# An encoder layer on one core: one RG-LRU pair moved behind the last head group, the first residual's affine per column block, three shared PSUM banks for small products, small loads on GpSimd's queue

## The chip, the core and the metric

The kernel runs on one core of one Trainium2 chip. A core has TensorE (PE in the profile, its weight loads PEld), VectorE (DVE), ScalarE (ACT), GpSimd (POOL) and SyncE (SP). Each executes its own list of instructions in order; they wait for one another through semaphores. SP, ACT and POOL also issue DMAs. SBUF holds the working tiles; PSUM, eight banks, takes the matmuls' results. The metric is the device time of one execution in microseconds (us); lower is better.

## The reference

One post-norm layer for 256 positions of width 2048, in fp32:

```
h  = LN(x)
z  = h @ w_in                                # u, gate | r,k,v + three small | gA | gB
yA = gelu(gate) * RGLRU(conv(u))             # 16 heads of 128: a linear scan in time
yB = RWKV7(r, k, v, decay, a, g)             # 32 heads of 64: a delta-rule recurrence
h  = LN1(ALPHA*h + (sig(gA)*yA + sig(gB)*yB) @ w_out)
h  = LN2(ALPHA*h + CrossAttn(h, mem))        # 4 heads, 256 memory tokens
h  = LN3(ALPHA*h + (silu(h@wg) * (h@wu)) @ wd)
```

The change touches the mixer (the second to fifth line) and the start of the fifth.

## The kernel before

**Weight tiles.** Every large product reads its weights once, in pieces of 128 x 1024 fp32 (512 KB). `split_half` (L148) loads a piece into `raw` from SP's queue (L152), lets ScalarE round it to `wh` (L155) and VectorE form the rest `wl` (L157). PE multiplies both parts: `wstat` (L162) with eight matmuls of 512 columns (L168) and eight of 256 (L171) a piece; `xstat` (L189), where the activations are the stationary side, with twelve of 512 (L202, L203, L206). A piece is called a unit below. `wtile` (L178) makes one tile of 128 output columns from two units, and ScalarE and VectorE join its two halves from PSUM (L183, L186: `jl`, `js`). `raw` has four buffers, `wh` and `wl` three, the accumulators two.

**Order.** The program is written in one order, and a planner makes from it, before the run, each engine's fixed list: among the instructions that it takes to be ready, the one of lowest priority number goes first. `stream` gives the weight pieces and their evacuations numbers by unit, ahead of all other work; `ahead` gives some loads the first place. `defer(n, fn)` (L79) writes `fn` into the program only after n more units, so small products fall between weight tiles. A new tile in a buffer waits until everything that used the old one is done.

**The mixer's loop** (L758) runs over four groups of four tiles (eight heads) of RWKV7. Per group:
- `rwkv_group` (L407): twelve weight tiles (k, r, v for each of four tiles, 24 units). Their small work (`tile_stage`, L437) goes into `kkr`, `gt`, `bkt` and `sv`, which have one buffer each for all groups; `zk`, `zr`, `zv` have two. The norm of the keys is a product in a bank of the pool `mixps` (L447), as are the two products of L502 that L506 masks into `gt`.
- three units later `recurrence` (L522): a triangular solve on VectorE in 31 steps (L547, L550), then DMAs that put its result into `ymat`. `PACE[g]` units after that, `chunk_steps` (L562): `x1z` (L565), small products into the pool `recps` (L571 to L628), and at its end the normalisation (L635 to L646), transposes (L655) and gate products (L662) with the weights `lwg`.
- `gate_group` of the group before (L735): four weight tiles, 8 units, with `yar` loaded back from DRAM.
- two `lru_pair`s (L668): six weight tiles each, 12 units, for two heads of the RG-LRU. The recurrent gates (L671) are two products into `lrups` (L674), a pool of one bank, read by ScalarE (L676, L678) into `rr` and `ii`, two buffers each; the scans (L722) follow five units behind the pair.
- the decay rates of the next group (L382) after 7 and 10 units, and their exponentials at the end of the second pair (`late`).

So the order is rwkv 0, pairs 0 and 2, rwkv 1, gate 0, pairs 4 and 6, rwkv 2, gate 1, pairs 8 and 10, rwkv 3, gate 2, pairs 12 and 14, gate 3. PSUM: two banks `mixps`, three `recps`, two accumulators, one `lrups`.

**After the loop** the twelve finished tiles of y are loaded as `yr` (L779, POOL's queue), behind the last chunk steps, whose memory they take. The residual `hres` is loaded (L801, POOL), scaled and shifted by the first LayerNorm's rows in `affine_rows` (L266): eight blocks of 256 columns, two buffers of `gb`, sixteen loads of 128 KB from ACT's queue (L272), 32 operations on VectorE (L274, L275). W_out is four column blocks of eight units; after each, `residual` (L790) adds the product. `mraw` (L814) loads the memory tokens for the attention into the tags vh0 and vh1.

Of the kernel before, what the change touches and what calls it, by code (L numbers as in the profile page):

```python
# [18 lines left out]
P = 128  # L19
# [8 lines left out]
NT = 16  # L28
NG = 4
DR = (7, 10)  # L30
PACE = (20, 28, 28, 16)
NB0, NB1 = 3, 5
XP, CP = 4, 5
ALPHA = float(2.0 ** 0.25)
# [12 lines left out]
def trunk(ctx, tc, x, memT, vec, rows, consts, lruw, loraw, w_in, w_out, wq, wk, wv, wo, wgu, wd, out,  # L47
# [4 lines left out]
    def dump(name, t):  # L52
        if name in dbg:
            nc.gpsimd.dma_start(dbg[name], t)
# [188 lines left out]
    def layer_norm(pre, st, gname, bname, psum, xh, xl, small, tags):  # L243
        mom = [ln_rstd(small, st, tt) for tt in range(2)]
        for nb in range(4):
# [7 lines left out]
            for k in range(4 * nb, 4 * nb + 4):  # L253
# [9 lines left out]
                eng = nc.gpsimd if k % 4 == 3 else nc.vector  # L263
                eng.tensor_tensor(xl[k], full, xh[k].bitcast(F32), ALU.subtract)

    def affine_rows(pre, gi, name):  # L266
        with tc.tile_pool(name=name, bufs=2) as pool:
            for nb in range(8):
                s = slice(nb * 256, (nb + 1) * 256)
                gb = pool.tile([P, 2, 256], F32, name="gb")  # L270
                for n in range(2):
                    nc.scalar.dma_start(gb[:, n, :], rows[gi + n:gi + n + 1, s].broadcast_to([P, 256]))  # L272
                for tt in range(2):
                    nc.vector.tensor_tensor(pre[:, tt, s], pre[:, tt, s], gb[:, 0, :], ALU.mult)  # L274
                    nc.vector.tensor_tensor(pre[:, tt, s], pre[:, tt, s], gb[:, 1, :], ALU.add)  # L275
# [7 lines left out]
    y_d = [dram.tile([P, T], F32, name=f"y_d{k}") for k in range(NT)]  # L283
    at = ExitStack()
    with ExitStack() as mx:
        mp = mx.enter_context(tc.tile_pool(name="mixps", bufs=2, space=PSUM))
        rp = mx.enter_context(tc.tile_pool(name="recps", bufs=3, space=PSUM))
        accs[0] = mx.enter_context(tc.tile_pool(name="accs", bufs=2, space=PSUM))
        lp = mx.enter_context(tc.tile_pool(name="lrups", bufs=1, space=PSUM))
        wk1 = mx.enter_context(tc.tile_pool(name="wk1", bufs=1, side="right"))  # L290
        bx = ExitStack()
        boot = bx.enter_context(tc.tile_pool(name="boot", bufs=1))
# [89 lines left out]
        def decay_rates(g, jp, rates):  # L382

            if jp == 0:
                rates.append(grp.tile([P, 4, T], F32, name="avg"))
                rates.append(grp.tile([P, 4, T], F32, name="evg"))
            avg, evg = rates
            lw = wk1.tile([P, 2, 2, P], F32, name="lw")
            nc.sync.dma_start(lw, loraw[2 * g + jp, :, 0:2])
            for n, dst in ((0, evg), (1, avg)):  # L390
                ps = mps()
                for jj in range(2):
                    nc.tensor.matmul(ps[:, jj * T:(jj + 1) * T], lw[:, n, jj, :], lo[n], start=True, stop=True)
                nc.scalar.activation(dst[:, 2 * jp:2 * jp + 2], ps.rearrange("p (j t) -> p j t", j=2), AF.Sigmoid)
            for j in range(2 * jp, 2 * jp + 2):
                nc.vector.tensor_tensor_scan(evg[:, j], cmask, evg[:, j], 0.0, ALU.mult, ALU.add)

        def decay_exps(avg, evg):
            dm = grp.tile([P, 4, 4], F32, name="dm", bufs=2)
            ev4 = evg.rearrange("p j (c t) -> p j c t", c=4)  # L400
            for j in range(4):
                nc.scalar.activation(dtg[:, j, :, 1:65], ev4[:, j], AF.Exp, scale=-CDEC)
            nc.vector.tensor_copy(dm, dtg[:, :, :, 64])
            nc.scalar.activation(evg, evg, AF.Exp, scale=CDEC)
            return avg, evg, dm
# [156 lines left out]
        def chunk_steps(g, kkr, gt, bkt, sv, dm, yb, gi):  # L562
# [85 lines left out]
            for j in range(4):  # L648
                i = 4 * g + j
                fs = slice(j * P, (j + 1) * P)  # L650
                lw = wk1.tile([P, 2, P], F32, name="lwg", bufs=2)
                nc.sync.dma_start(lw, loraw[i // 2, :, 2:4, i % 2])
                ps = rps()
                for a in range(2):
                    last = nc.tensor.transpose(ps[:, a * P:(a + 1) * P], ot[a][:, fs], ident)  # L655
                on = wk1.tile([P, T], F32, name="on", tag="A")
                nc.scalar.activation(on, ps[:, 0:T], AF.Identity, scale=col("gn_g", i), bias=col("gn_b", i))
                nc.vector.tensor_tensor(on, on, yb[:, j, :], ALU.add)
                ps = rps()
                with tc.issue_after(last.ins):  # L660
                    for a in range(2):
                        nc.tensor.matmul(ps[:, 0:T], lw[:, a, :], lo[2 + a], start=(a == 0), stop=(a == 1))  # L662
                nc.vector.tensor_tensor(yb[:, j, :], on, ps[:, 0:T], ALU.mult)
# [4 lines left out]
        def lru_pair(i0, late=None):  # L668
            st = []

            def recurrent_gates(i, uc, lrw):  # L671
                ps = lp.tile([P, 512], F32, name="lrups")
                for n in range(2):
                    nc.tensor.matmul(ps[:, n * T:(n + 1) * T], lrw[:, n, :], uc, start=True, stop=True)  # L674
                rr = wk1.tile([P, T], F32, name="rr", bufs=2)
                nc.scalar.activation(rr, ps[:, 0:T], AF.Sigmoid, bias=col("ba", i))  # L676
                ii = wk1.tile([P, T], F32, name="ii", bufs=2)
                nc.scalar.activation(ii, ps[:, T:2 * T], AF.Sigmoid, bias=col("bx", i))  # L678
                nc.vector.tensor_tensor(ii, ii, uc, ALU.mult)
                th = wk1.tile([P, T], F32, name="th", bufs=2)  # L680
                nc.scalar.activation(th, rr, AF.Tanh, scale=sp8[:, i:i + 1])
                st.append((i, rr, ii, th))

            for i in (i0, i0 + 1):
                lrw = wk1.tile([P, 2, P], F32, name="lrw", bufs=2)
                nc.sync.dma_start(lrw, lruw[:, i])
                ua = wk1.tile([P, T], F32, name="ur", tag="ge", bufs=2)
                wtile(w_in[52 + 3 * i], xTh, xTl, out=ua)
                uc = wk1.tile([P, T], F32, name="uc", bufs=2)
                with stream(32):  # L690
                    evac[0] = nc.scalar.activation(uc, ua, AF.Identity, scale=col("conv3", i),
                                                   bias=col("conv_b", i))
                    for s in (1, 2, 3):
                        nc.vector.scalar_tensor_tensor(uc[:, s:T], ua[:, 0:T - s], col(f"conv{3 - s}", i),
                                                       uc[:, s:T], ALU.mult, ALU.add)
                defer(4, partial(recurrent_gates, i, uc, lrw))
# [38 lines left out]
        def gate_group(g, yb):  # L735
            for j in range(4):
                i = 4 * g + j
                gb = wtile(w_in[100 + i], xTh, xTl)
                sb = wk1.tile([P, T], F32, name="sb", bufs=2)
                with stream(32):  # L740
                    nc.scalar.activation(sb, gb, AF.Sigmoid)
                nc.vector.tensor_tensor(sb, sb, yb[:, j, :], ALU.mult)
                yr = wk1.tile([P, T], F32, name="yar", bufs=2)
                with ahead():
                    nc.sync.dma_start(yr, ya_d[i])
                nc.vector.tensor_tensor(yr, sb, yr, ALU.add)
                if g < NG - 1:
                    with ahead():
                        nc.sync.dma_start(y_d[i], yr)
                else:  # L750
                    split_to(yr, yh[i], yl[i])
                dump(f"y{i}", yr)
# [4 lines left out]
            decay_rates(0, jp, rates)  # L757
        for g in range(NG):  # L758
            yb = rwkv_group(g, PACE[g], *(rates if g else decay_exps(*rates)))
            if prev is not None:  # L760
                gate_group(g - 1, prev)
            if g < NG - 1:
                rates, full = [], []
                defer(DR[0], partial(decay_rates, g + 1, 0, rates))
                defer(DR[1], partial(decay_rates, g + 1, 1, rates))
                lru_pair(4 * g)
                lru_pair(4 * g + 2, late=lambda: full.append(decay_exps(*rates)))
                rates = full[0]
            prev = yb
        lru_pair(NT - 4)  # L770
# [19 lines left out]
    def residual(nb, pt, st):  # L790
        for tt in range(2):
            s = hres[:, tt, nb * 512:(nb + 1) * 512]
            nc.vector.scalar_tensor_tensor(s, s, ALPHA, pt[tt], ALU.mult, ALU.add)
            ln_stats(st, hres, tt, nb)

    with at:
        ap_ = at.enter_context(tc.tile_pool(name="attn", bufs=1, reuse_waits="tile"))
        sm_ = at.enter_context(tc.tile_pool(name="attns", bufs=1, reuse_waits="tile"))
        for nb in range(4):
            s = slice(nb * 512, (nb + 1) * 512)  # L800
            nc.gpsimd.dma_start(hres[:, :, s], h0_d[:, :, s])  # L801
        affine_rows(hres, 0, "gb0")
        dump("h0", hres)
        st = ap_.tile([P, 2, 4, 6], F32, name="st1")
        for nb in range(4):
            pt = xstat([w_out[nb, u] for u in range(4)], yh, yl)
            residual(nb, pt, st)
        dump("pre1", hres)
        layer_norm(hres, st, "g1", "b1", mp, xTh, xTl, sm_, ("f0", "f1", "f2"))
# [223 lines left out]
```

## Time and profile before

| | us |
|---|---|
| median of three runs | 2167.06 |
| lowest and highest | 2162.23, 2167.65 |
| the profiled execution, of which the profile is | 2165.43 |
| its span, first to last instruction | 2163.6 |

| engine | busy, us |
|---|---|
| PE | 2085.8 |
| PEld | 1789.3 |
| DVE | 1476.9 |
| ACT | 1092.3 |
| POOL | 80.6 |

The profile is of one execution, its times in us from the first instruction. In a list of waits the columns are total, count and longest. In a table by stretches, each engine's busy time is followed by its number of instructions; the last three columns are the granted TensorE clock (1.00 is full speed), the DMA engines' busy share and GB/s. In a timeline the columns are start, duration, engine, line and operation, and in brackets the idle time before it and what ended it. In a list of groups the numbers behind the bar are busy us, mean ns, idle us before. A list of DMA issues ends with KB and the median us to landing.

### The profile page before, as it was taken

Reading aid. Unit: us, or ns where it says so; the run is one execution under the profiler, and the core shown is the slowest. Engines: PE = TensorE matmul, PEld = TensorE weight load, DVE = VectorE, ACT = ScalarE, POOL = GpSimd, SP = SyncE. Lnnn points to the kernel's source line nnn. Section 1 sums busy time; section 2 is a strip of 40 time slices with the busy share of each in tenths; the row PEclk is TensorE's granted clock in tenths of the full one; section 3 lists DMA queues with packets and bytes.
Section 4 is the critical chain, followed back from the end, with each engine's and each line's share of the span. In section 5 each row is a group of like instructions: output and inputs, shape, how many; then the busy total and the mean of one; then the engine's idle time right before and its main releaser. Section 6 shows DMA issues by size and latency. Waiting matters only on the chain.

```text
span 2163.6 us, 31791 instructions
## 1 busy us (share of the span) xinstructions
PE 2085.8 (96%) x12176; PEld 1789.3 (83%) x12176; DVE 1476.9 (68%) x2357; ACT 1092.3 (50%) x1656; POOL 80.6 (4%) x104
## 2 busy tenths in 40 slices
PE   7999999999999999988999999999999999999996
PEld 6888888888888888867878888788888888888885
DVE  7788877978796879667765565585555555544445
ACT  6756645565556555644644444355444444443332
POOL 1100010010001000110000000000000000000001
PEclk9999999999999999999999999999999999999998
DMA  8645535544554455467565544566555555555553
GB/s 287 198 156 178 173 108 158 178 142 151 159 182 133 150 162 194 132 215 238 186 207 192 170 140 166 192 204 202 187 187 192 187 188 192 186 192 193 193 192 125
DMA packets 148376, 387.75 MB, mean 179 GB/s; under 512 B 38784, under 2 KB 58112, under 8 KB 147712
## 3 DMA queue, kind: packets, MB, share of 16 engines
q1 hardware_dynamic: 137776, 368.81, 51.5%
q10 hardware_dynamic: 9296, 13.24, 2.3%
q0 software_dynamic: 1152, 3.67, 0.5%
q8 instruction: 95, 1.56, 0.3%
q14 instruction: 57, 0.47, 0.1%
HBM read 375.05 MB, written 10.62 MB: 178 GB/s over the span
## 4 chain that ended last, share of the span: by engine, by line
PE 82%; DVE 10%; DMA 4%; ACT 3%; issue 2%; POOL 0%; SPq 0%; ACTq 0%; DVEq 0%; POOLq 0%
PE acc L168 34%; PE acc L171 17%; PE acc L206 7%; PE acc L202 7%; PE acc L203 7%; DVE wl L157 4%; DMA gb<-in_rows_dram 2%; ACT wh L155 1%; DVE pd L547 1%; DVE xi L550 1%; PE rec L603 1%; PE rec L610 1%; PE rec L628 1%; PE mix L502 1%; PE rec L662 1%
## 5 line engine op out<-in xcount | busy, mean ns | idle before, releaser
L157 DVE TENSOR_TENSOR wl<-raw,wh 128x1024 fp32r<-128x1024 f32 x656 | 801.7, 1223 | 524.1 <-ACT wh L155 496.2
L155 ACT CAST wh<-raw 128x1024 fp32r<-128x1024 f32 x656 | 685.8, 1047 | 666.3 <-PE acc L203 262.4
L168 PE MATMUL acc<-xT,wh 128*128 128x512 f32 x3520 | 917.1, 399 | 5.7 <-DVE js L186 4.0
L168 PEld LDWEIGHTS acc<-xT,wh 128*128 128x128 f32 x3520 | 636.2, 190 | 123.8 <-DVE js L186 4.7
L171 PEld LDWEIGHTS acc<-xT,wl 128*128 128x128 f32 x3520 | 484.0, 191 | 36.0
L171 PE MATMUL acc<-xT,wl 128*128 128x256 f32 x3520 | 503.0, 284 | 0.0
L203 PE MATMUL acc<-wh,f 128*128 128x512 f32 x352 | 136.9, 389 | 0.0
L202 PE MATMUL acc<-wh,f 128*128 128x512 f32 x352 | 136.9, 389 | 0.0
L206 PE MATMUL acc<-wl,f 128*128 128x512 f32 x352 | 108.4, 389 | 0.0
L183 ACT COPY jl<-acc 128x256 f32<-128x256 f32 x236 | 86.6, 367 | 22.0 <-PE acc L171 20.1
L186 DVE TENSOR_TENSOR js<-acc,jl 128x256 f32<-128x256 f32 x215 | 90.0, 419 | 3.4 <-ACT jl L183 3.1
L206 PEld LDWEIGHTS acc<-wl,f 128*128 128x128 f32 x352 | 66.1, 188 | 13.7
L202 PEld LDWEIGHTS acc<-wh,f 128*128 128x128 f32 x352 | 66.1, 188 | 13.7
L203 PEld LDWEIGHTS acc<-wh,f 128*128 128x128 f32 x352 | 66.0, 188 | 13.7
L616 POOL TENSOR_SCALAR dms<-ct,dm 128x128 f32<-128x128 f32 x48 | 36.4, 771 | 787.3 <-DVE smat L622 712.7
L547 DVE TENSOR_TENSOR pd<-xi,al 128x2 f32<-128x2 f32 (+30 forms) x124 | 63.2, 510 | 2.5
L203 PE MATMUL acc<-wh,A 128*128 128x512 f32 x128 | 50.5, 396 | 0.5 <-DVE A L212 0.5
L202 PE MATMUL acc<-wh,A 128*128 128x512 f32 x128 | 50.3, 394 | 0.3 <-ACT A L211 0.3
L202 PE MATMUL acc<-wh,oT 128*128 128x512 f32 x128 | 50.0, 391 | 0.0
L203 PE MATMUL acc<-wh,oT 128*128 128x512 f32 x128 | 49.8, 389 | 0.0
L203 PE MATMUL acc<-wh,B 128*128 128x512 f32 x128 | 49.8, 389 | 0.0
L202 PE MATMUL acc<-wh,B 128*128 128x512 f32 x128 | 49.8, 389 | 0.0
(260 smaller groups left out, 2095.7 us busy)
## 6 DMA issues: line engine op xcount, KB each, us to landing
raw<-in_w_in_dram SPq DMA_DIRECT2D x232, 512.0 KB, 3.5
raw<-in_wgu_dram SPq DMA_DIRECT2D x176, 512.0 KB, 3.4
raw<-in_wd_dram SPq DMA_DIRECT2D x88, 512.0 KB, 3.6
raw<-in_wk_dram SPq DMA_DIRECT2D x32, 512.0 KB, 4.3
raw<-in_w_out_dram SPq DMA_DIRECT2D x32, 512.0 KB, 4.6
raw<-in_wv_dram SPq DMA_DIRECT2D x32, 512.0 KB, 3.5
raw<-in_wq_dram SPq DMA_DIRECT2D x32, 512.0 KB, 3.4
raw<-in_wo_dram SPq DMA_DIRECT2D x32, 512.0 KB, 3.4
```

The costliest lines, as they stand in the source:

```text
L155: nc.scalar.copy(h, raw)
L157: nc.vector.tensor_tensor(l, raw, h.bitcast(F32), ALU.subtract)
L168: nc.tensor.matmul(acc, w, both[id(xh[k])], start=(k == 0), stop=False)
L171: mm = nc.tensor.matmul(acc[:, 0:T], l[:, kk * P:(kk + 1) * P], xh[k], start=False, stop=(k == 15))
L183: nc.scalar.copy(t, a[:, T:2 * T])
L186: nc.vector.tensor_tensor(out, a[:, 0:T], t, ALU.add)
L202: nc.tensor.matmul(pt[tt], xh[k][:, ts], w, start=(first and kk == 0), stop=False)
L203: nc.tensor.matmul(pt[tt], xl[k][:, ts], w, start=False, stop=False)
L206: nc.tensor.matmul(pt[tt], xh[k][:, ts], l[:, kk * 512:(kk + 1) * 512], start=False, stop=(last and kk == 1))
L502: nc.tensor.matmul(pt[hh][:, c * P:(c + 1) * P], q["bk"][rows, c, :], kr[rows, c, :], start=True, stop=True)
L547: nc.vector.tensor_tensor(pd[:, 0:nj, 0:t + 1], xi[:, 0:nj, 0:t + 1], al[:, 0:t + 1, t].rearrange("p (o s) -> p o s", o=1) .broadcast_to([ ...
L616: nc.gpsimd.tensor_scalar(dms[:, j * P:(j + 1) * P], smask, dm[:, j, c:c + 1], None, ALU.mult)
```

## The change

Four things:
1. Pair 10 (heads 10 and 11) is issued after the tiles of group 3 and ahead of gate 2, in place of the second pair after gate 1. The exponentials for group 3 then hang on pair 8. `PACE` of groups 2 and 3 becomes 20.
2. The recurrent gates' products use `mixps`, which gets three banks; `lrups` is gone. `recps` is opened first and so has the banks ahead of it.
3. The loads of `lw`, `lwg`, `lrw` and `yar` are issued by GpSimd, not SP.
4. `affine_rows` for the first residual is replaced by two loads of whole rows, 1 MB each, spread over the partitions, from GpSimd's queue into the tags vh0 and vh1, and by `affine_block`, four operations of 512 columns ahead of each block's residual.

```
-PACE = (20, 28, 28, 16)
+PACE = (20, 28, 20, 20)
...
+    def affine_block(pre, g, b, nb):
+        s = slice(nb * 512, (nb + 1) * 512)
+        for tt in range(2):
+            nc.vector.tensor_tensor(pre[:, tt, s], pre[:, tt, s], g[:, s], ALU.mult)
+            nc.vector.tensor_tensor(pre[:, tt, s], pre[:, tt, s], b[:, s], ALU.add)
...
-        mp = mx.enter_context(tc.tile_pool(name="mixps", bufs=2, space=PSUM))
         rp = mx.enter_context(tc.tile_pool(name="recps", bufs=3, space=PSUM))
+        mp = mx.enter_context(tc.tile_pool(name="mixps", bufs=3, space=PSUM))
         accs[0] = mx.enter_context(tc.tile_pool(name="accs", bufs=2, space=PSUM))
-        lp = mx.enter_context(tc.tile_pool(name="lrups", bufs=1, space=PSUM))
...
-            nc.sync.dma_start(lw, loraw[2 * g + jp, :, 0:2])
+            nc.gpsimd.dma_start(lw, loraw[2 * g + jp, :, 0:2])
...
-                nc.sync.dma_start(lw, loraw[i // 2, :, 2:4, i % 2])
+                nc.gpsimd.dma_start(lw, loraw[i // 2, :, 2:4, i % 2])
...
-                ps = lp.tile([P, 512], F32, name="lrups")
+                ps = mps()
...
-                nc.sync.dma_start(lrw, lruw[:, i])
+                nc.gpsimd.dma_start(lrw, lruw[:, i])
...
-                    nc.sync.dma_start(yr, ya_d[i])
+                    nc.gpsimd.dma_start(yr, ya_d[i])
...
             yb = rwkv_group(g, PACE[g], *(rates if g else decay_exps(*rates)))
+            if g == NG - 1:
+                lru_pair(NT - 6)
             if prev is not None:
                 gate_group(g - 1, prev)
...
-                lru_pair(4 * g)
-                lru_pair(4 * g + 2, late=lambda: full.append(decay_exps(*rates)))
+                exps = lambda: full.append(decay_exps(*rates))
+                if g < NG - 2:
+                    lru_pair(4 * g)
+                    lru_pair(4 * g + 2, late=exps)
+                else:
+                    lru_pair(4 * g, late=exps)
...
-        affine_rows(hres, 0, "gb0")
-        dump("h0", hres)
+        gb0 = []
+        for n in range(2):
+            b = ap_.tile([P, 2048], F32, name="gb0", tag=f"vh{n}")
+            nc.gpsimd.dma_start(b, rows[n:n + 1, :].broadcast_to([P, 2048]))
+            gb0.append(b)
         st = ap_.tile([P, 2, 4, 6], F32, name="st1")
         for nb in range(4):
             pt = xstat([w_out[nb, u] for u in range(4)], yh, yl)
+            affine_block(hres, gb0[0], gb0[1], nb)
             residual(nb, pt, st)
```

## The prediction

> **What bounds the kernel now.** I read the page first, then PE's waits, then its stalls in slices of 4 us, then the timeline around each.
>
> ```profile
> span 2163.6 us, 31791 instructions
> PE 2085.8 (96%) x12176; PEld 1789.3 (83%) x12176; DVE 1476.9 (68%) x2357; ACT 1092.3 (50%) x1656; POOL 80.6 (4%) x104
> ```
>
> TensorE (PE) is the bound, and no part of the change takes matmuls out. What can be won is PE's idle time, 77.8 us, and the half-clock time behind each idle stretch. PE's waits, with total, count and longest in us, name the idle time:
>
> ```profile
> PE lrups L674 <- ACT ii L678: 12.2, 4, 3.6
> PE rec L662 <- DMA lwg<-in_loraw_dram: 7.4, 3, 6.4
> PE acc L206 <- DVE wl L157: 6.1, 4, 3.9
> PE acc L168 <- DVE js L186: 4.0, 3, 1.9
> PE mix L447 <- DVE gt L506: 3.4, 7, 0.5
> PE rec L655 <- DVE ott L646: 2.7, 1, 2.7
> ```
>
> All six lie in the mixer or in the W_out product. The unit of the argument is half a weight tile, split, multiplied and counted once:
>
> ```profile
> 663.33 2.00 PE L168 MATMUL acc<-xT,wh 128*128 128x512 f32 x8
> 665.17 1.11 PE L171 MATMUL acc<-xT,wl 128*128 128x256 f32 x8
> 666.12 2.00 PE L168 MATMUL acc<-xT,wh 128*128 128x512 f32 x8
> ```
>
> A unit takes 666.12 - 663.33 = 2.79 us and holds eight L168 matmuls, so L168 counts divided by 8 count units. The moved pair is 6 tiles, 12 units, 33.5 us of PE; it is only put elsewhere.
>
> **Third bank for the small products.** The recurrent gates' second product waits until ScalarE has read the first from the only lrups bank, and ScalarE is late because rr, two deep, waits for the scans of the pair before. Slices (PE's busy time first, DVE's third, then PEclk):
>
> ```profile
> 224.00:228.00 4.00, 1.57 (x5) 1.30 (x5) 4.00 (x7) 2.87 (x7) 0.00 (x0) 0.69 0.43 143
> 228.00:232.00 4.00, 4.00 (x15) 3.52 (x14) 3.84 (x7) 2.20 (x4) 0.00 (x0) 0.50 0.65 217
> 660.00:664.00 4.00, 4.00 (x17) 3.32 (x17) 2.71 (x6) 1.74 (x3) 0.00 (x0) 0.70 0.88 237
> 872.00:876.00 4.00, 4.00 (x18) 3.44 (x18) 2.58 (x5) 2.30 (x4) 0.00 (x0) 0.75 0.94 223
> 600.00:660.00 60.00, 54.02 (x298) 46.97 (x297) 58.65 (x108) 36.37 (x62) 0.00 (x0) 0.99 0.56 171
> ```
>
> Stalls 12.2 us plus slow clock behind three of them, 4 x (0.50 + 0.30 + 0.25) = 4.2: at most 16.4 us. With three shared banks the second product no longer waits for the first one's reader. But VectorE (DVE) is full in these stretches (58.65 of 60), its order is fixed, and the next wl comes when it comes; and the chunk steps behind stand just in time:
>
> ```profile
> 879.12 0.70 DVE L565 STREAM_TRANSPOSE x1z<-ymat 32x512 f32<-32x512 f32 x1
> 879.88 1.20 PE L571 MATMUL rec<-x1z,gt 128*32 128x32 f32 x32
> ```
>
> x1z is ready at 879.82 and PE uses it at 879.88: a PE that comes earlier waits here. I take half, **-8** (0 to -16.4). The key norm's wait (L447 on gt) is one for a mix bank; a third bank removes it: **-3** (0 to -3.4). That a gate now holds a mix bank while it waits for rr costs nothing, as two others stay free and L447's stage uses two.
>
> **The pair moved behind the last head group.** What it is to cover is the end of the mixer, where the last chunk steps run almost alone:
>
> ```profile
> 880.00:932.00 52.00, 20.08 (x72) 12.51 (x72) 1.00 0.41 130
> 932.00:947.00 15.00, 0.00 (x0) 0.00 (x0) 0.77 0.75 263
> 934.72 1.46 SPq L652 DMA_DIRECT2D lwg<-in_loraw_dram  x2
> 936.00:940.00 4.00, 0.00 (x0) 0.00 (x0) 2.36 (x6) 2.63 (x5) 0.00 (x0) 0.86 1.03 395
> 940.00:944.00 4.00, 1.62 (x4) 1.38 (x5) 0.00 (x0) 0.00 (x0) 0.00 (x0) 0.50 0.57 197
> 944.00:948.00 4.00, 3.20 (x10) 1.99 (x10) 3.27 (x9) 2.39 (x7) 0.00 (x0) 0.79 0.34 94
> ```
>
> The first two rows hold L168 alone: 72/8 = 9 units are left when the chunk steps of group 3 begin at 880, and none from 932 on. Then PE waits 2.7 us for the norm (L655) and 6.4 us for the gate weights lwg (L662), and runs at half clock: 9.1 us of waits, and 1.62 x 0.50 + 3.20 x 0.21 = 1.5 of clock, 10.6 in all. After the change 12 + 8 + 12 + 12 + 8 = 52 units follow group 3's tiles instead of 40, and chunk steps that start at a like distance find about 20 units. What is late next is lwg again: it is issued from GpSimd (POOL) behind 12 yr and 4 hres loads, so a few us of its wait may stay. I take **-7.5** (0 to -10.6).
>
> The cost is at the other end. Group 2 loses 12 units of cover, so its chunk steps fall into group 3's tiles:
>
> ```profile
> 566.00:669.00 103.00, 64.09 (x243) 44.75 (x242) 0.98 0.60 180
> 661.00 1.44 DVE L565 STREAM_TRANSPOSE x1z<-ymat 32x512 f32<-32x512 f32 x2
> 669.00:708.00 39.00, 12.16 (x41) 6.99 (x42) 1.00 0.33 107
> 252.17 1.20 PE L571 MATMUL rec<-x1z,gt 128*32 128x32 f32 x32 [0.22 <-DVE x1z L565]
> 289.63 0.45 DVE L475 TENSOR_TENSOR kkr<-zr,dtg 128x128 f32<-128x128 f32 x1 [1.31 <-PE rec L598]
> 280.00:300.00 20.00, 20.00 (x166) 17.17 (x165) 13.74 (x25) 8.89 (x14) 4.92 (x8) 1.00 0.24 81
> 740.00:760.00 20.00, 19.49 (x121) 16.59 (x121) 16.97 (x31) 10.13 (x17) 0.00 (x0) 1.00 0.38 132
> L157 DVE TENSOR_TENSOR wl<-raw,wh 128x1024 fp32r<-128x1024 f32 x656 | 801.7, 1223 | 524.1 <-ACT wh L155 496.2 <-PE acc L171 17.2 <-ACT rhsz L606 3.0
> ```
>
> Between 566 and 669 PE did 243/8 = 30 units; group 2's chunk steps then begin, x1z ready since 662.4. Gate group 1 and one pair are 20 units, so now they begin 9 to 10 units into group 3 (the new pace of 3 + 20 is no later bound). Group 3 may not write kkr, gt, bkt and sv, single buffers, until they are read: in group 0 the first write to kkr stood behind L598, 289.63 - 252.17 = 37 us after the start. In such a stretch PE also does 41/8 = 5 units, so the release comes at unit 15. The k, r and v tiles are two deep: the third r is due at unit 16. It just fits. But DVE, 16.97 of 20 us busy in a tile's plain stretch, then has two tiles' held work to catch up (its splits, wl, are 1.22 us each), so I charge **+3** (0 to +25, below). On the other side, group 2's solve gets no second pair beside it, and so loses one of the four lrups stalls, counted above.
>
> SP loses the loads lw, lwg, lrw and yar, and POOL gets them. Of these only lwg stands among the waits above; the others are issued long ahead. POOL's queue is short:
>
> ```profile
> L779 POOL DMA_DIRECT2D yr<-y_d x12: 537/538/739, 924.4 to 930.4; - x12
> lwg<-in_loraw_dram SPq DMA_DIRECT2D x16, 128.0 KB, 2.7
> yr<-y_d POOLq DMA_DIRECT2D x12, 128.0 KB, 4.1
> hres<-h_d POOLq DMA_DIRECT2D x4, 512.0 KB, 8.0
> gb<-in_rows_dram ACTq DMA_DIRECT2D x2, 1024.0 KB, 6.8
> ```
>
> The landing is 4.1 us against 2.7 for 128 KB, 1.4 later, with units to cover it: 0 (-2 for a freer SP, to +4).
>
> **A rule against it.** The Trainium skill, "SBUF — State Buffer", section "Who interferes with whom", says that descriptors of a GpSimd-issued load are not written while VectorE runs in a two-port mode, and advises the SP or ACT queue; the section on the bandwidth pool has 0.62 us grow to 3.1. By the page, an estimate: eight pairs of lwg 2.5 us late each, 20 us, and the sum would be near zero. The twelve yr issues above, 537 to 739 ns beside a working VectorE, show at most 0.2 us of it, and the page itself excepts operations with two inputs, as wl is. The sum keeps 0; the rule stands beside the third rival.
>
> **Affine per column block.**
>
> ```profile
> L274 DVE TENSOR_TENSOR hres<-hres,gb 128x256 f32<-128x256 f32 x48 | 19.3, 433 | 15.5 <-DMA gb<-in_rows_dram 13.3 <-issue 2.2
> 984.00:988.00 4.00, 2.57 (x9) 2.06 (x10) 4.00 (x6) 1.35 (x3) 0.00 (x0) 0.83 0.95 266
> 988.00:992.00 4.00, 4.00 (x15) 3.18 (x14) 4.00 (x10) 2.48 (x7) 0.00 (x0) 0.74 0.96 342
> ```
>
> Before, VectorE's queue stops again and again for 128 KB gb pieces, wl stands behind, and L206 loses 6.1 us plus 2.57 x 0.17 + 4.00 x 0.26 = 1.5 of clock: 7.6. Now 32 operations of 256 columns become 16 of 512, and two loads of 1 MB are waited for at most once each. The end of the mixer holds their place (tags vh), so they land about 8 to 12 us into W_out, an estimate from 8.0 and 6.8; the first residual needs them after 8 units, 22 us. If VectorE's order asks earlier, wl waits, with two spare units (5.6 us) before PE does. I take **-5** (-7.6 to +6). mraw now waits for the last block; 32 units of W_out cover its load, and none is charged.
>
> **Sum.** -8 - 3 - 7.5 + 3 + 0 - 5 = -20.5 us. The profiled execution took 2165.43 (span 2163.6 and 1.8 around it); it lies 1.6 under the median of the three runs. So 2165.4 - 20.5 = **2145**.
>
> **Rivals.** (1) *VectorE keeps the rhythm.* In the full stretches a vanished lrups stall becomes a wait for wl, js or x1z, and half of L447's too: the -8 and 1.5 of the -3 are lost. For it: DVE 58.65 of 60. Against: after 660 DVE has room (2.71 of 4) and PE still ran slow. Time: 2145 + 8 + 1.5 = 2154.5.
>
> (2) *Slower: group 3 stands behind group 2's chunk steps.* If the tiles run dry at unit 12 rather than 16, PE does 2.5 units instead of 5 in the chunk stretch (7 us idle), then waits for two tiles' held work: a tile's 16.97 less six wl of 1.22 leaves 9.6, and the joins are not held, so about 7 a tile, an estimate, and 14 us for two; 2 us of half clock; and the third solve starts 23 us later, which brings back the mixer's bare end, 7.5. That is 30.5 for the 3 charged: 2145 + 27.5 = 2172. It decides at the point where kkr's release passes unit 16. Against it: group 0's steps reach into group 1's tiles too, and PE waited 0.22 us at their start and was busy 20.00 of 20 from 280 to 300.
>
> (3) *POOL's loads come late.* lwg then lands between yr's 1.4 and hres's 5.3 us after the old 2.7, say 3 us that PE waits in each of the first three groups, and behind yr and hres in the last, where half of the 7.5 is lost: 2145 + 9 + 4 = 2158. For it: POOL issues in order, behind its own work and waits. Against: its issues above are steady. The Trainium skill's "SBUF — State Buffer" would have it so.
>
> (4) *Everything is covered*: all of the stalls go, nothing new: 2165.4 - 16.4 - 3.4 - 10.6 - 7.6 = 2127.
>
> **How the numbers follow.** Forecast 0.58 (2135 to 2152), rival 1 0.15, rival 2 0.10, rival 3 0.07, rival 4 0.10. A change under 0.3% (6.5 us) is what a measurement here can't tell from none. Faster: 0.58 + 0.10, 0.12 of rival 1 and 0.03 of rival 3 = 0.83; same: 0.03 + 0.04 and 0.03 of rival 2 = 0.10; slower 0.07. Range 2130 to 2162: it leaves out rival 2 and the ends of 4 and 3.
>
> **What would show it.** Right: no wait at the gates' product over 1 us; L447 gone from PE's waits; main units (L168) running beside the last L662; one idle stretch at most on L274's successor. Wrong: PE idle inside group 3's first two tiles with the releaser L598 or L628, or DVE; L662 waiting over 4 us for lwg; L206 waiting for wl with VectorE stopped at gb0. The sum is wrong altogether if the compiled order of VectorE shifts the solve, whose end sets when the chunk steps start.

## The result and the profile after

The changed kernel takes 2144.44 us (median of 4 runs, 2141.4 to 2147.81), the kernel before 2166.11 beside it (4 runs, 2162.23 to 2167.65): a ratio of 0.990 [0.9887, 0.9913]. Forecast was 2145.0. The profiled execution took 2147.81 us. Below, a ratio is also given in us, as its distance from 1 times 2166.1: here -21.7 [-24.5, -18.8].

The page of the changed kernel, its head:

```profile
span 2146.0 us, 31754 instructions
PE 2078.3 (97%) x12176; PEld 1782.4 (83%) x12176; DVE 1472.4 (69%) x2341; ACT 1092.3 (51%) x1658; POOL 117.4 (5%) x162
```

PE's idle time, span less busy, went from 77.8 to 2146.0 - 2078.3 = 67.7 us, and its busy time fell by 7.5 with the same 12176 matmuls. Together these are the 17.6 us by which the span is shorter.

Most of the 7.5 us is not slow clock. The products that are masked into `gt` (L502, now L507; 16 a tile, 256 in all) took PE 23.84 us and now take 18.59, 5.3 less. Eight of the sixteen go into one bank of `mixps`, eight into another. Two rows of the kernel before and one of the changed kernel:

```profile
360.02 1.16 PE L502 MATMUL mix<-kkr,bk 64*128 64x128 f32 x8
362.45 1.16 PE L502 MATMUL mix<-kkr,bk 64*128 64x128 f32 x8
...
357.18 1.16 PE L507 MATMUL mix<-kkr,bk 64*128 64x128 f32 x16
```

Where the two halves alternate, all sixteen take 1.16 us, as long as eight of one half alone. With two banks PE's list puts one half behind the other in 6 of the 16 tiles; with three, in none. The rest is about what the clock gives, an estimate: PE's busy time times the missing share of the clock, added up over slices of 4 us, fell from 14.2 to 11.6 us.

PE's waits in the changed kernel (line numbers are 5 higher than before in the mixer, so L576 is the old L571 and L667 the old L662):

```profile
PE acc L168 <- DVE m L330: 11.0, 2, 7.0
PE rec L576 <- DVE x1z L570: 10.5, 3, 4.4
PE acc L168 <- DVE js L186: 7.7, 6, 2.4
...
PE acc L202 <- ACT wh L155: 2.9, 1, 2.9
PE rec L667 <- DMA lwg<-in_loraw_dram: 2.4, 4, 0.8
...
PE acc L206 <- DVE wl L157: 1.0, 1, 1.0
```

Everything the change aimed at is gone or small: lrups (12.2), the key norm's L447 (3.4) and L655 (2.7) are no longer listed, lwg fell from 7.4 to 2.4, L206 from 6.1 to 1.0. That is 12.2 + 3.4 + 2.7 + 5.0 + 5.1 = 28.4 us of waits. Against it stand x1z with 10.5, js with 3.7 more (7.7 from 4.0) and wh with 2.9. The new rows are the subject of the experiments. (The m row, 9.0 before, lies in the start-up, which the change does not touch.)

### The profile page after: what moved, and what is told of

Same layout as the page of the kernel before. It is cut to its first block, busy times and chain, and to the rows that moved or that the text cites. A ratio compares the mean times of both kernels' runs of the same rounds, so it can differ in the third digit from the quotient of the medians.

```text
span 2146.0 us, 31754 instructions
## 1 busy us (share of the span) xinstructions
PE 2078.3 (97%) x12176; PEld 1782.4 (83%) x12176; DVE 1472.4 (69%) x2341; ACT 1092.3 (51%) x1658; POOL 117.4 (5%) x162
## 4 chain that ended last, share of the span: by engine, by line
PE 81%; DVE 10%; DMA 4%; issue 2%; ACT 2%; SPq 0%; POOL 0%; ACTq 0%; DVEq 0%; POOLq 0%
PE acc L168 33%; PE acc L171 17%; PE acc L206 7%; PE acc L202 7%; PE acc L203 7%; DVE wl L157 3%; DVE pd L552 1%; DMA gb<-in_rows_dram 1%; ACT wh L155 1%; DVE xi L555 1%; PE rec L608 1%; PE rec L633 1%; PE rec L615 1%; DMA mraw<-in_memT_dram 1%; PE mix L507 1%
## 5 line engine op out<-in xcount | busy, mean ns | idle before, releaser
L168 PE MATMUL acc<-xT,wh 128*128 128x512 f32 x3520 | 914.3, 399 | 10.0 <-DVE js L186 7.7
L168 PEld LDWEIGHTS acc<-xT,wh 128*128 128x128 f32 x3520 | 636.6, 190 | 128.8 <-DVE js L186 9.4
L206 PE MATMUL acc<-wl,f 128*128 128x512 f32 x352 | 108.4, 389 | 0.0
L183 ACT COPY jl<-acc 128x256 f32<-128x256 f32 x236 | 86.5, 367 | 24.5 <-PE acc L171 23.8
L203 PEld LDWEIGHTS acc<-wh,f 128*128 128x128 f32 x352 | 66.1, 188 | 13.8
L206 PEld LDWEIGHTS acc<-wl,f 128*128 128x128 f32 x352 | 66.1, 188 | 13.7
L913 ACT ACTIVATE fsg<-js 128x256 f32<-128x256 f32 x44 | 18.4, 417 | 55.7 <-DVE js L186 55.5
```

The lines of the kernel that those rows point to most:

```text
L168: nc.tensor.matmul(acc, w, both[id(xh[k])], start=(k == 0), stop=False)
L183: nc.scalar.copy(t, a[:, T:2 * T])
L203: nc.tensor.matmul(pt[tt], xl[k][:, ts], w, start=False, stop=False)
L206: nc.tensor.matmul(pt[tt], xh[k][:, ts], l[:, kk * 512:(kk + 1) * 512], start=False, stop=(last and kk == 1))
```

## Where the new waits stand

x1z is the solve's result, written to DRAM, read back and transposed; the chunk steps (L576) begin with it. Rows of the changed kernel's timeline at group 2's chunk steps and, in the last two, at group 3's:

```profile
636.19 0.69 DVE L555 TENSOR_REDUCE xi<-pd 128x16 f32<-128x512 f32 x1
636.91 1.27 SPq L558 DMA_DIRECT2D scx<-xi  x2
641.80 1.99 SPq L563 DMA_DIRECT2D ymat<-scx  x4
647.41 0.70 DVE L570 STREAM_TRANSPOSE x1z<-ymat 32x512 f32<-32x512 f32 x1
648.17 1.72 PE L576 MATMUL rec<-x1z,gt 128*32 128x32 f32 x32 [3.97 <-DVE x1z L570]
...
847.75 0.70 DVE L570 STREAM_TRANSPOSE x1z<-ymat 32x512 f32<-32x512 f32 x1 [2.71 <-DMA ymat<-scx]
848.51 1.92 PE L576 MATMUL rec<-x1z,gt 128*32 128x32 f32 x32 [4.43 <-DVE x1z L570]
```

The solve's last reduction ends at 636.9; its result is in x1z at 648.1, 11 us later. The four loads of L563 are issued from 641.80 to 643.30 and land 2.4 to 2.7 us after that, so by 646.0; the transpose begins at 647.41, behind other work in VectorE's list. So some 9 of the 11 us are the way through DRAM. At group 3 VectorE itself stands idle for the loads, 2.71 us. PE's queue already has L576 next: the list was fixed before the run, as if x1z were there by now, and the main products behind L576 can't pass it. So PE waits 3.97 us here and 4.43 us at group 3's steps (last row). Slices of 4 us around both (columns as in the prediction):

```profile
644.00:648.00 4.00, 0.20 (x1) 0.00 (x0) 3.90 (x8) 1.44 (x2) 0.54 (x1) 1.00 0.89 178
648.00:652.00 4.00, 3.83 (x37) 3.37 (x38) 1.95 (x3) 0.00 (x0) 0.00 (x0) 0.57 0.89 342
844.00:848.00 4.00, 0.08 (x1) 0.00 (x0) 1.29 (x2) 3.82 (x7) 0.00 (x0) 0.81 0.91 192
848.00:852.00 4.00, 3.49 (x36) 3.13 (x37) 3.97 (x8) 0.60 (x1) 0.00 (x0) 0.50 0.94 369
585.00:648.00 63.00, 57.76 (x320) 49.51 (x319) 61.80 (x125) 37.99 (x63) 2.16 (x4) 1.00 0.57 177
```

Each wait drags a slice at about half clock behind it: 3.83 x 0.43 + 3.49 x 0.50 = 3.4 us. The two heads cost 8.4 + 3.4 = 11.8 us. The last row shows with what the solve shares VectorE (third busy time): in the 63 us ahead of the chunk steps it has 1.2 us free, with solve, splits and gates in one queue. Whether x1z is late or PE early is seen below, beside a kernel without the move (e8).

## The experiments

Two theories. **A:** the parts add up, each by the stall that it removes. **B:** two parts (the moved pair, GpSimd's loads) remove the same stall at the end of the mixer, and the move pays for it again where the chunk steps begin. First each part alone on the kernel before, all on one chip, where that took 2167.83 us.

**Banks alone** (e1_banks)

```diff
-        mp = mx.enter_context(tc.tile_pool(name="mixps", bufs=2, space=PSUM))
         rp = mx.enter_context(tc.tile_pool(name="recps", bufs=3, space=PSUM))
+        mp = mx.enter_context(tc.tile_pool(name="mixps", bufs=3, space=PSUM))
-        lp = mx.enter_context(tc.tile_pool(name="lrups", bufs=1, space=PSUM))
...
-                ps = lp.tile([P, 512], F32, name="lrups")
+                ps = mps()
```

> Only the PSUM part of the change, on the kernel before: gates' products in mixps, three banks, no lrups. My theory: the four waits of the gates' second product (12.2 us) and the key norm's wait on gt (3.4) go, but some of the 16.4 us that hung on them comes back as waits for x1z at the head of the chunk steps: 2165.4 - 8 - 3, that is about 2155 (2151 to 2160). Rival, VectorE keeps the rhythm: nearly all of it comes back as waits for x1z, js or wl; 2160 to 2166. Rival, everything is covered: 2147.

Measured: 2150.66 us, ratio 0.9928 [0.9914, 0.9942], -15.6 us [-18.6, -12.6]. Rows of its waits:

```profile
PE rec L661 <- DMA lwg<-in_loraw_dram: 6.8, 2, 6.4
PE rec L570 <- DVE x1z L564: 6.7, 2, 3.3
PE acc L168 <- DVE js L186: 6.6, 4, 2.2
PE acc L206 <- DVE wl L157: 4.9, 3, 2.6
```

lrups is gone, and x1z and js have taken part of its place, lwg and L206 stay. The products into gt take 18.59 us here as well (L501), against 23.84. Still this is the largest part of the gain, and more than the 11 us forecast.

**The moved pair alone, with its PACE** (e2_move)

```diff
-PACE = (20, 28, 28, 16)
+PACE = (20, 28, 20, 20)
...
+            if g == NG - 1:
+                lru_pair(NT - 6)
...
-                lru_pair(4 * g)
-                lru_pair(4 * g + 2, late=lambda: full.append(decay_exps(*rates)))
+                exps = lambda: full.append(decay_exps(*rates))
+                if g < NG - 2:
+                    lru_pair(4 * g)
+                    lru_pair(4 * g + 2, late=exps)
+                else:
+                    lru_pair(4 * g, late=exps)
```

> Only the moved pair and its PACE, on the kernel before, with lrups still one bank. My theory: the bare end of the mixer goes (10.6 us), one of the four lrups waits goes with the pair that no longer stands beside the second solve, and 3 to 8 us come back as waits around the second and third chunk steps: 2156 to 2161. Rival, the move needs the third bank: nothing won, 2163 to 2170. Rival, group 3 stands behind the second chunk steps: over 2170, with PE idle inside group 3's first two tiles.

Measured: 2167.59 us, ratio 1.0006 [0.9995, 1.0017]: nothing. Rows of its waits:

```profile
PE acc L168 <- DVE js L186: 8.4, 7, 1.8
PE rec L571 <- DVE x1z L565: 6.7, 3, 3.5
PE lrups L674 <- ACT ii L678: 6.5, 2, 3.3
PE acc L206 <- DVE wl L157: 6.1, 3, 2.3
PE rec L662 <- DMA lwg<-in_loraw_dram: 6.0, 2, 5.4
```

L655 is gone and lrups halved, 2.7 + 5.7 us, but x1z comes in with 6.7 and js with 4.4 more. And lwg keeps its long wait, 5.4 us, although main products now follow the chunk steps: cover for PE does not bring the weights any earlier. SP issues this lwg at 910.47, behind POOL's yr and hres loads (this kernel's timeline):

```profile
899.18 6.57 POOL L785 DMA_DIRECT2D yr<-y_d  x12 [14.11 <-PE rec L628]
907.27 2.84 POOL L807 DMA_DIRECT2D hres<-h_d  x4 [1.52 <-ACT wh L155]
910.47 0.38 SPq L652 DMA_DIRECT2D lwg<-in_loraw_dram  x1
918.96 2.05 PE L662 MATMUL rec<-lo,lwg 128*128 128x256 f32 x4 [5.36 <-DMA lwg<-in_loraw_dram]
```

**The affine alone** (e3_affine): the diff's `affine_block` and its two loads in place of `affine_rows(hres, 0, "gb0")`, on the kernel before.

> Only the affine per column block with its two 1 MB loads, on the kernel before. My theory: the waits of L206 for wl in W_out (6.1 us and 1.5 of slow clock) fall to one stop of about 3 us: 2159 to 2163. Rival, the loads come late behind the bare end of the mixer, since they wait for the same memory: the stop is longer, 2164 to 2170.

Measured: 2157.23 us, ratio 0.9955 [0.9941, 0.9968], -9.7 us [-12.8, -6.9]. L206 stands no longer among the waits; those of the mixer stay, and grow a little in this profile (lrups 13.7, lwg 8.8, x1z 2.5).

**GpSimd's loads alone** (e4_pool)

```diff
-            nc.sync.dma_start(lw, loraw[2 * g + jp, :, 0:2])
+            nc.gpsimd.dma_start(lw, loraw[2 * g + jp, :, 0:2])
...
-                    nc.sync.dma_start(yr, ya_d[i])
+                    nc.gpsimd.dma_start(yr, ya_d[i])
```

(and likewise lwg and lrw)

> Only the small loads lw, lwg, lrw, yar on GpSimd's queue instead of SP's, on the kernel before. My theory: nothing on the path, within 3 us of the kernel before, 2163 to 2168; L662's wait for lwg at the end stays, 6 to 9 us. Rival, POOL's loads come late: 2171 to 2180, with L662 waiting for lwg over 2 us in every group. Rival, a freer SP feeds raw earlier: 2160 or less.

Measured: 2159.57 us, ratio 0.9966 [0.9953, 0.9978], -7.4 us [-10.2, -4.8]. Rows of its waits:

```profile
PE acc L206 <- DVE wl L157: 9.3, 2, 6.4
PE rec L662 <- DMA lwg<-in_loraw_dram: 3.3, 4, 1.3
```

The part that was forecast at nothing wins what the move was forecast to win: the list has lwg at 3.3 for 7.4, its longest wait 1.3 for 6.4, and L655 gone (L206 is up by 3.2 in this profile). In the changed kernel POOL issues as follows (start, duration):

```profile
904.14 0.76 POOL L657 DMA_DIRECT2D lwg<-in_loraw_dram  x1 [25.65 <-PE rec L660]
905.23 0.73 POOL L657 DMA_DIRECT2D lwg<-in_loraw_dram  x1 [0.33 <-PE rec L667]
905.96 6.41 POOL L790 DMA_DIRECT2D yr<-y_d  x12
912.36 2.88 POOL L812 DMA_DIRECT2D hres<-h_d  x4
```

In one queue lwg goes ahead of yr and hres, because it comes first in the program (in e4 too: 929.95 and 931.04, yr from 931.76); from two queues it came behind them. The rival of a freer SP, 2160 or less, fits the time as well: the raw loads of w_in land no sooner (3.6 us in the median, 3.5 before), but how the 7.4 us divide between the two causes is not shown.

**The changed kernel without the move** (e8_nomove; f2_nomove is the same kernel again, on the chip of f1_after, the changed kernel again)

```diff
-PACE = (20, 28, 20, 20)
+PACE = (20, 28, 28, 16)
...
-            if g == NG - 1:
-                lru_pair(NT - 6)
...
+                lru_pair(4 * g)
+                lru_pair(4 * g + 2, late=lambda: full.append(decay_exps(*rates)))
```

> The changed kernel without the moved pair: old order, old PACE, but three mix banks, affine per block and GpSimd's small loads. New theory N: the move is a loss here; it gives its price back at the bare end only, and that end is already mended by lwg on GpSimd's queue. The parts alone gave 17, 11 and 8 us; with 2 to 6 us that more than one of them claims, 2134 to 2140, below the changed kernel. My prediction's terms: the move is worth 4.5 us, so without it 2147 to 2151.

> The changed kernel itself, to stand on one chip beside the next three: 2141 to 2147.

> The changed kernel without the moved pair and with the old PACE once more, on the chip of the changed kernel. Theory N: the move costs 3 to 8 us, so this is that much below the changed kernel. Rival, the difference seen was between chips: within 2 us of it. The prediction's term: 4.5 us above it.

Measured: e8, which has the old PACE too, 2140.22 us (2138.3 to 2142.09), ratio 0.9883 [0.9865, 0.9900]. On the other chip f1, with the move, 2147.44 (2142.6 to 2152.42), 0.9916 [0.9898, 0.9935], and f2, without it, 2140.46 (2137.95 to 2144.75), 0.9885 [0.9864, 0.9906]. Twice the kernel without the move is ahead, by 0.0017 (3.7 us, the first pair of ratios, on two chips) and 0.0031 (6.7 us, on one chip). The intervals overlap, so the size is loose; that the move wins 4.5 us in place is out. So is e2's rival, that the move would win if it had the third bank. Rows of e8's waits, and of its timeline at group 2's chunk steps:

```profile
PE rec L576 <- DVE x1z L570: 5.9, 2, 3.3
PE acc L168 <- DVE js L186: 4.4, 3, 2.1
...
PE rec L667 <- DMA lwg<-in_loraw_dram: 2.6, 4, 1.2
...
656.25 1.92 PE L576 MATMUL rec<-x1z,gt 128*32 128x32 f32 x58
```

The end of the mixer is mended without a pair behind it: lwg 2.6, longest 1.2, L655 not listed. x1z and js cost 10.3 here and 18.2 with the move. That is theory B.

At group 2 the solve is no later with the move: its last reduction ends at 636.9 us in the changed kernel and at 636.7 in e8. But e8, like the kernel before, begins the chunk steps after 1416 matmuls of L168 (177.0 units), without a wait; the changed kernel after 1386 (173.2 units). PE comes 3.8 units earlier there. The place follows PACE: 1400 with 26 for group 2 (e5 below), 1448 with 32 (e6).

**The small loads back on SP** (e9_nopool): the inverse of e4's diff, on the changed kernel.

> The changed kernel with the small loads on SP's queue again. Theory: lwg is late again behind raw and the residual's loads, one wait of L662 of about 5 us with slow clock behind it although pair 14 and gate 3 could cover it: 2147 to 2153. Rival, the prediction's term of nothing: 2142 to 2146.

Measured: 2148.34 us, ratio 0.992 [0.9902, 0.9939], beside f1's 0.9916 on the same chip: no difference. Yet in its trace the wait is back:

```profile
PE rec L667 <- DMA lwg<-in_loraw_dram: 5.3, 2, 4.7
```

A wait of 4.7 us lies about at the edge of what these intervals (4 us each way) can tell; the trace settles who makes lwg late, the times do not settle what it is worth beside the move.

**Group 2's chunk steps later** (e6_late): rival 2 of the prediction, sought by force.

```diff
-PACE = (20, 28, 20, 20)
+PACE = (20, 28, 32, 20)
```

> The changed kernel with PACE of group 2 at 32: its chunk steps begin 15 units into group 3, and kkr comes free near unit 20, past the point (unit 16) from which my second rival decides. Rival 2 then holds: PE idle in group 3's second or third tile behind L598's and L628's successors or VectorE, 2152 to 2170. Against it, the planner fills PE with pair 10's units: no such idle time, 2139 to 2147.

Measured: 2144.16 us, ratio 0.9898 [0.9878, 0.9918], the same as the changed kernel's 0.990. The chunk steps begin at 671.2 in place of 648.2, and group 3's first write to kkr moves from 685.8 to 704.0. A join of group 3 does wait for it (ScalarE's row), but PE has other work throughout (the stretch of the chunk steps; from 640 to 780 its longest stop is 2.03 us, for lwg):

```profile
671.00:711.00 40.00, 40.00 (x466) 34.93 (x465) 21.14 (x38) 14.53 (x23) 8.65 (x13) 1.00 0.23 79
705.02 0.51 ACT L371 ACTIVATE zr<-js,omu 128x256 f32<-128x256 f32 x1 [2.32 <-DVE kkr L481]
```

So group 3 behind kkr's release has some 18 us to spare beyond what the change uses. The x1z wait of this head is gone too, but the time is not lower: x1z keeps 4.8 us at the other heads, and the key norm's product (L452) waits 3.7 us for ScalarE in group 3's first tile, at 637.3, which it did not before.

**The chunk steps of groups 0, 2 and 3 later** (e5_pace), and, to separate it from the move, the same without the move (f3_nomove_pace: e8's diff with PACE (26, 28, 28, 26) and the same two lines).

```diff
-PACE = (20, 28, 20, 20)
+PACE = (26, 28, 26, 33)
...
         lru_pair(NT - 4)
+        lru_pair(NT - 2)
         gx.close()
...
-        lru_pair(NT - 2)
         flush()
```

> The changed kernel with PACE (26, 28, 26, 33) and, so that the last chunk steps can be that late, pair 14 issued ahead of the residual's allocation. Theory: the chunk steps are planned 2 to 4 us before VectorE has the solve ready; two units later the three waits for x1z (10.5 us and some 3 of slow clock) go: 2131 to 2138. Rival, VectorE keeps the rhythm: the time comes back as waits for js and wl: 2141 to 2148.

> The changed kernel without the moved pair, with PACE (26, 28, 28, 26) and pair 14 issued ahead of the residual's allocation, so that the chunk steps of groups 0 and 3 are planned some 2 units later. Theory: the two x1z waits (5.9 us, 1 to 2 of slow clock) go, and no others come: 2131 to 2136, the best of all. Rival: with no pair behind group 3 the later chunk steps lengthen the bare end by as much as they save: 2138 to 2143.

Measured: e5 2136.85 us (2131.32 to 2137.56), ratio 0.9864 [0.9844, 0.9884], -29.5 us: the fastest with the whole solve. On the same chip it is 3.4 us below e8, and their runs do not overlap (e8 from 2138.3). f3 2141.82, 0.9893 [0.987, 0.9915], no better than f2 beside it (2140.46). Three places in the timeline of e5:

```profile
636.49 0.70 PE L452 MATMUL mix<-sq,ct 128*128 128x256 f32 x2 [3.73 <-ACT sq L450]
652.39 1.43 DVE L570 STREAM_TRANSPOSE x1z<-ymat 32x512 f32<-32x512 f32 x2
653.75 2.11 PE L576 MATMUL rec<-x1z,gt 128*32 128x32 f32 x64
827.01 0.70 DVE L570 STREAM_TRANSPOSE x1z<-ymat 32x512 f32<-32x512 f32 x1 [1.20 <-DMA ymat<-scx]
841.39 1.79 PE L576 MATMUL rec<-x1z,gt 128*32 128x32 f32 x54
```

Group 2's x1z arrives just as PE comes to it, at 653.8; group 3's is there at 827.7 and PE takes it at 841.4, with main products between; no x1z wait is left in this kernel's list, and js is down to 3.9. But the key norm's product now waits for ScalarE, 5.5 us in two stops: the first row stands 17 us ahead of group 2's chunk steps, in place of the 3.97 us there. And at group 3 it is the solve that is earlier: it begins at 761.9 us, after 1591 matmuls of L168, in the changed kernel at 776.8, after 1619. The chunk steps are put back by less, from 1793 to 1808. What holds group 3's solve in the changed kernel is not shown.

So among these kernels the moved pair wins only together with these edits, and later paces win nothing without the pair: in f3, too, a stop for ScalarE (2.9 us) stands where group 0's x1z wait was, and group 3's chunk steps stay where e8 has them, 232.0 units in, with 2.6 us of wait.

**Half of the solve** (e7_solve). The kernel leaves out every second step of the solve, so its results are not the layer's; it shows what the solve's length and its load on VectorE cost together.

```diff
-            for t in range(1, 32):
+            for t in range(1, 32, 2):
```

> The changed kernel with every second step of the triangular solve left out (16 of 31, half of VectorE's work on it). Theory: VectorE's load beside the solve makes the waits for x1z (10.5 us) and js (7.7), so both go nearly whole, with their slow clock: 2122 to 2130. Rival, the way of the solve's result through DRAM is what is late: the x1z waits stay, 2136 to 2144.

Measured: 2116.24 us, ratio 0.9781 [0.9754, 0.9807], -47.4 us, by the ratios 26 below the changed kernel. x1z and js are no longer listed, and a stretch ahead of the chunk steps reads

```profile
573.00:618.00 45.00, 45.00 (x255) 39.62 (x254) 39.40 (x76) 24.71 (x41) 1.61 (x3) 1.00 0.65 200
```

PE 45.00 of 45.00, VectorE 39.40 of 45 where it was 61.80 of 63. The way through DRAM is unchanged in this kernel, 11.2 us at group 2 (602.1 to 613.3), and does no harm, since the solve is done sooner: it takes 28.7 us in place of 51.9. Whether the whole solve on an emptier VectorE would do as well is not shown. In the profiled executions, 32.5 us apart, PE's idle time falls by 18.7 us, about x1z's 10.5 and js's 7.7 together, and its busy time by 13.8; 9.1 of that is slow clock (added up as above, from 11.6 to 2.5 us).

## Why the prediction was right, and where it was not

The time and its sign were right, the sum in its parts was not: alone, three parts won more than their terms, and the fourth, the move, won nothing alone and cost time in place. That these errors cancelled to about 1 us is luck.

| term | forecast, us | part alone, us | in place |
|---|---|---|---|
| third bank (-8 and -3) | -11 | -15.6 [-18.6, -12.6] | not run |
| moved pair (-7.5 and +3) | -4.5 | +1.3 [-1.1, +3.7] | +3.7 and +6.7 (after over e8, f1 over f2) |
| GpSimd's loads | 0 | -7.4 [-10.2, -4.8] | -0.9 (f1 over e9), within the interval |
| affine | -5 | -9.7 [-12.8, -6.9] | not run |
| sum | -20.5 | -31.4 | -21.7 measured |

- **Third bank.** Right: the gates' product waits nowhere, L447 on gt is gone, and part of the gain came back as waits for x1z and js, as "a PE that comes earlier waits here" said. Mis-sized: 11 was taken and 15.6 measured. The prediction held that idle time and half-clock time are what can be won; 5.3 us of the part lie in busy time that it put at nothing, the products into gt, which a third bank lets alternate.
- **"What is late next is lwg again: it is issued from GpSimd (POOL) behind 12 yr and 4 hres loads."** Wrong, and the root of two wrong terms. lwg goes ahead of both. So the loads, charged at 0, mend the end of the mixer by themselves (lwg and L655 fall by 6.8 us in e4's list, though L206 grows by 3.2), and the -7.5 was a stall that another part of the same diff had already removed. The move alone couldn't have won it either: with cover, lwg still waited 5.4 us (e2).
- **"+3" for VectorE's catch-up.** Not where it was put: PE did not stand idle behind kkr's release, not even when that came 18 us later (e6). By the lists of waits the price of the move lies at the hand-over from solve to chunk steps: x1z and js, 18.2 us with the move and 10.3 without. The step that failed is "now they begin 9 to 10 units into group 3 (the new pace of 3 + 20 is no later bound)": it took the start from where x1z had been ready, but the list follows PACE, and PE came 3.8 units sooner and waited. So one sign of being wrong did come: PE idle in group 3's first two tiles behind DVE, 3.97 us for x1z. The price is not shown wait by wait: e6, without this wait, is no faster. And since group 3's solve begins 28 matmuls of L168 later than in e5, some catch-up of VectorE may stand behind the 4.43 us at group 3; no run separates this. The prediction had quoted the very rows (x1z at 879.82, PE at 879.88), and drew from them a limit to the banks' gain only, not a price of the move.
- **Affine.** Right in mechanism; the size was 9.7 for 5. Alone, L206's wait vanished entirely; the two loads were in time. In the changed kernel one stop for wh, 2.9 us, and 1.0 at L206 stay.
- **Rivals.** Rival 1 (VectorE keeps the rhythm) was half true: x1z 10.5 and js 7.7 are its waits, but the banks outweigh them. Rival 2's idle time did not occur, nor under e6's force. Rival 3, late loads from POOL, did not occur; the list of DMA issues of the changed kernel, with the median us to landing in the last column:

```profile
lw<-in_loraw_dram POOLq DMA_DIRECT2D x8, 256.0 KB, 3.5
lrw<-in_lruw_dram POOLq DMA_DIRECT2D x16, 128.0 KB, 3.6
lwg<-in_loraw_dram POOLq DMA_DIRECT2D x16, 128.0 KB, 2.7
yar<-ya_d POOLq DMA_DIRECT2D x16, 128.0 KB, 3.0
```

From SP the same four took 3.6, 3.7, 2.7 and 3.6. The Trainium skill, "SBUF — State Buffer", section "Who interferes with whom", lets GpSimd's writing of descriptors be held up while VectorE works in a two-port mode; these rows, from a mixer in which VectorE is 61.80 of 63 us busy in one stretch, show no sign of it. How much of VectorE's work here is in that mode was not counted.

**Open.** Three parts alone without the move sum to -32.7 us (15.6 + 7.4 + 9.7), together they gave -25.3 and -24.9: 7 to 8 us are claimed twice among them, or lie in the intervals (3 us each); no run separates this. Nor is it settled which of e5's edits (three paces, the last pair ahead of the residual's buffers) does the most, nor what the banks and the affine are worth in place.

## What to carry to other kernels

Price a part of a change by what is left when the other parts are in: two edits that point at the same stall win it once, and the second one brings only its cost. Work that is moved to cover one hole uncovers another: look for the hand-over whose producer is the fullest engine (here the solve's result), and check where the fixed list now puts its consumer. Where one small load is late behind bulk ones from another queue, put it into that queue ahead of them before bringing cover for the wait.

## What the runs showed of the hardware that was not expected

- A 128 KB load issued by GpSimd lands in 2.7 us, as one from SP does, with 0.73 us of issuing for 0.38 on SP (medians). Issued behind yr and hres at the end of the mixer it took 7.5 us (before) to 8.8 (e2), ahead of them 2.7 (e4) to 3.5 (the changed kernel). So here the order of issues went with the wait; order and issuer were not changed one without the other.
- The solve's result (xi, 128 x 512 numbers), sent to DRAM and read back in another layout, takes 11 us from its last reduction to the transposed tile (636.9 to 648.1; 837.6 to 848.5 at group 3), about 9 of it in DMA at group 2. That is four main units of PE.
- Sixteen products of 64 rows each, alternating between the two halves of the partitions and two banks, take PE 1.16 us; the eight of one half alone take 1.16 us too, and both halves one after the other 1.90 us (L502 at 320.18 in the kernel before).
